# Lowering the place of the TensorE transposes in the attention stretch of a hybrid decoder layer

## The chip, the cores and the metric

The kernel runs on one core of a Trainium2 chip. The metric is device time in microseconds of one execution. Before the change the median of three runs is 2443.2 us (2442.11 to 2446.67).

## What is computed

One layer of a decoder over 2048 prompt rows and 8 decode rows of width 1024, all in float32. The stretch that the change touches is the first part: RMSNorm, one input projection into q, k, v and the convolution branch, banded attention with a window of 128 and sinks, and the causal convolution of width 31.

```python
z = rms_norm(x, norm_mix_g) @ w_in
q, k, v, cu = jnp.split(z, [Q_END, K_END, V_END], axis=-1)
q = rope(rms_norm(q.reshape(B, T, N_HEADS, HEAD_DIM), q_norm_g), pos)
k = rope(rms_norm(k.reshape(B, T, N_KV_HEADS, HEAD_DIM), k_norm_g), pos)
s = jnp.einsum('bnqkgd,bnjkd->bnkgqj', qb, kk) * ATTN_SCALE   # blocks of 128 queries, 256 keys
pr = sink_softmax_weights(s, mask, sink)
o = jnp.einsum('bnkgqj,bnjkd->bnqkgd', pr, vv)
a, g = jnp.split(cu, 2, axis=-1)
glu = a * jax.nn.sigmoid(g)
conv_o = jax.nn.silu(layer_norm(causal_dwconv(conv_ext, conv_w, conv_b), conv_ln_g, conv_ln_b))
h = x + jnp.concatenate([attn_o, conv_o], axis=-1) @ w_out
# then a gated ConvFFN (width 2816) and a gated per-layer embedding, each with its residual
```

## The kernel before

Every large product is made of three matmuls with operands split into a high and a low part (hi·hi, hi·lo, lo·hi; `mm3`, lines 195 to 197; the split is `hilo`, lines 212 and 213: a copy on ScalarE and a subtraction on VectorE).

The first 520 us or so work on the prompt in four quarters of 512 rows. A quarter consists of slots in an order written out by hand (`orders`): an "a" slot (`ag_unit`) is one 128-column piece of the convolution branch's projection, 24 matmuls of 512 columns; a "q" slot (`qkv_unit`) is the projection of one block of 128 rows to q, k and v, 24 matmuls of 512 and 24 of 256 columns (lines 820 to 825), and it starts a generator, `attn_block`, which is advanced slot by slot beside the projections. For one block `attn_block` does, a step per slot or two: transposes of q (four, line 596, tile qTp) and of k (two, line 599, tile kTp); scores of head group 0 (12 matmuls, line 621, tiles S); scores of head group 1; transposes of the probabilities of group 0 (two tiles PTp with four transposes each, line 648); the product with v (lines 659 to 662, tile O), beside it the transposes of group 1; the product of group 1. There are 16 blocks. `xn_k` transposes the normalized x of the next quarter (line 313, tile xT, four transposes for each 128 columns).

A matmul of scores contracts over a head's 64 dimensions only. It uses 64 of the 128 rows of the array: the even head of a pair the partitions 0 to 63, the odd head 64 to 127 (`rows = slice(par * 64, par * 64 + 64)`), each with a PSUM tile of its own. The loop issues the two in turn, even, odd, even, odd. In the order below, of two tiles S with neighbouring numbers, the lower number is the even head's. All transposes, projections and products with v contract over 128 rows.

All tiles of transposes and the product O rotate through one pool of two PSUM banks (`psT`, tag "T"); a buffer is free when `hilo` or a copy has read it.

The order on each engine is made when the program is built: a scheduler takes, among the instructions that it holds to be ready, the one with the lowest priority number. The number (`tc.cur_priority`) grows by one with each instruction that the program issues. The class `later(n)` raises it by n for the instructions in its body and takes it back behind them, so that these rank behind the next n instructions issued. It is already used at the layer norm's small matmuls (n = 60) and at a broadcast in the FFN stage. `bg` issues the convolution (line 411) in the background and puts the number back.

Of the kernel before, what the change touches and what calls it, by code (L numbers as in the profile page):

```python
# [33 lines left out]
def hybrid_layer_kernel(ctx: ExitStack, tc: tile.TileContext, I, O):  # L34
    nc = tc.nc
    DV, AC, GP, PE, SY = nc.vector, nc.scalar, nc.gpsimd, nc.tensor, nc.sync
# [29 lines left out]
    def ttile(name="T"):  # L66
        return psT.tile([128, 512], F32, tag="T", name=name)
# [100 lines left out]
    def col(src, c0):  # L168
        return src[:, :, c0:c0 + 128]
# [20 lines left out]
    for _ in range(4):  # L190
        for m in range(KD):
            W.add(col(w_gate, m * 128))

    def mm3(ps, wh, wl, xh, xl, first, last, more=False):
        PE.matmul(ps, wh, xh, start=first, stop=False, skip_group_check=more)  # L195
        PE.matmul(ps, wh, xl, start=False, stop=False, skip_group_check=more)  # L196
        PE.matmul(ps, wl, xh, start=False, stop=last, skip_group_check=more)  # L197

    def mm_tile(ps, hl, R, o, n):
        for k in range(KD):  # L200
            mm3(ps, hl[:, 0, k * 128:(k + 1) * 128], hl[:, 1, k * 128:(k + 1) * 128],
                R[k][:, 0, o:o + n], R[k][:, 1, o:o + n], k == 0, k == KD - 1)

    def mm_prod(ps, hl, c0, R, o, n, first):

        for k in range(4):
            w = slice(c0 + k * 128, c0 + (k + 1) * 128)
            mm3(ps, hl[:, 0, w], hl[:, 1, w], R[k][:, 0, o:o + n], R[k][:, 1, o:o + n],
                first and k == 0, k == 3, more=not first)

    def hilo(hi, lo, src):
        AC.copy(hi, src)  # L212
        DV.tensor_tensor(lo, src, hi.bitcast(F32), op=ALU.subtract)  # L213
# [11 lines left out]
    ident = const.tile([128, 128], F32, name="ident")  # L225
# [25 lines left out]
    xq = {}  # L251
# [56 lines left out]
    def xn_k(q, k):  # L308
        rt = r1_p.tile([128, 2, QT + NDEC], F32R, tag="r1", name="r1")
        g = gains[:, 0, k:k + 1]  # L310
        T = ttile("xT")
        for t in range(4):
            PE.transpose(T[:, t * 128:(t + 1) * 128], xq[q][t][:, k * 128:(k + 1) * 128], ident)
        AC.activation(rt[:, 0, :QT], T, func=AF.Identity, scale=g)
        DV.scalar_tensor_tensor(rt[:, 1, :QT], T, g, rt[:, 0, :QT].bitcast(F32), op0=ALU.mult, op1=ALU.subtract)
        if q == 3:
            xk = xdT.rearrange("p (b k) -> p b k", k=KD)[:, :, k]
            AC.activation(rt[:, 0, QT:], xk, func=AF.Identity, scale=g)
            DV.scalar_tensor_tensor(rt[:, 1, QT:], xk, g, rt[:, 0, QT:].bitcast(F32), op0=ALU.mult, op1=ALU.subtract)
        R1[q, k] = rt  # L320
# [13 lines left out]
    T = ttile("gT")  # L334
# [3 lines left out]
    for k in range(KD):  # L338
        xn_k(0, k)
    W.topup()  # L340
    T = ttile("cT")
# [46 lines left out]
    def conv_piece(conv_p, q):  # L388
# [22 lines left out]
                DV.scalar_tensor_tensor(co[c], t[:, i:i + QT], cvec[:, c, i:i + 1], co[c], op0=ALU.mult, op1=ALU.add)  # L411
                yield 610
        yield from layer_norm(conv_p, co, QT, 4, mixd[half], off)

    class later:


        def __init__(self, n):
            self.n = n

        def __enter__(self):
            tc.cur_priority += self.n

        def __exit__(self, *a):
            tc.cur_priority -= self.n

    def layer_norm(conv_p, co, n, ntt, dst, off):
        s = t_p.tile([128, QT], F32, tag="s", bufs=2, name="lns")[:, :n]
# [159 lines left out]
    def attn_block(b, pq, pkv):  # L588
        qn, kd, rs = qk_stage(b, pq, pkv)
        if b == 16:  # L590
            return
        yield 2
        qT = at_p.tile([128, 2, 4, 128], F32R, tag="qT", bufs=1, name="qT")
        T = ttile("qTp")
        for j in range(4):
            PE.transpose(T[:, j * 128:(j + 1) * 128], qn[:, j * 128:(j + 1) * 128], ident)
        T2 = ttile("kTp")
        for g in range(2):
            PE.transpose(T2[:, g * 128:(g + 1) * 128], kd[:, g].rearrange("p a d -> p (a d)"), ident)
        hilo(qT[:, 0].rearrange("p j t -> p (j t)"), qT[:, 1].rearrange("p j t -> p (j t)"), T)  # L600
        s = b % 2 + 1
        k2 = T2[:, :256].rearrange("p (g t) -> p g t", g=2)
        hilo(kTr[:, 0, :, s, :], kTr[:, 1, :, s, :], k2)
        yield 1
        den = at_p.tile([128, NH], F32, tag="den", bufs=2, name="den")
        mx = at_p.tile([128, NH], F32, tag="mx", bufs=2, name="mx")
        mv = mask[:, 0 if b else 1, :]
        Ps = {}

        def scores(g):  # L610
            P = at_p.tile([128, 4, 260], F32, tag="P", bufs=2, name="P")
            GP.tensor_copy(P[:, :, 256:257], sinkb[:, 4 * g:4 * g + 4].unsqueeze(2))
            Ps[g] = P
            S = [psS.tile([128, 2, 256], F32, tag="S", name="S") for _ in range(2)]

            for jj in range(2):
                j = 2 * g + jj
                for i, (a, e) in enumerate(((0, 1), (1, 0), (0, 0))):
                    for par in range(2):
                        rows = slice(par * 64, par * 64 + 64)  # L620
                        PE.matmul(S[par][:, jj, :], qT[rows, a, j, :],
                                  kTr[rows, e, g, s - 1:s + 1, :].rearrange("p a t -> p (a t)"),
                                  start=i == 0, stop=i == 2)
            for jj in range(2):
                for par in range(2):
                    h = 4 * g + 2 * jj + par
                    DV.tensor_tensor_reduce(out=P[:, 2 * jj + par, :256], in0=S[par][:, jj, :], in1=mv, scale=rs[:, h:h + 1],
                                            scalar=sinkb[:, h:h + 1], op0=ALU.add, op1=ALU.min, accum_out=mx[:, h:h + 1])
            for i in range(4):
                h = 4 * g + i  # L630
                AC.activation(P[:, i, :257], P[:, i, :257], func=AF.Exp, scale=-1.0, bias=mx[:, h:h + 1],
                              accum_out=den[:, h:h + 1])

        def normalize(g):
            g4 = slice(4 * g, 4 * g + 4)
            DV.reciprocal(den[:, g4], den[:, g4])
            for i in range(4):
                dn = den[:, 4 * g + i:4 * g + i + 1]
                AC.activation(Ps[g][:, i, :256], Ps[g][:, i, :256], func=AF.Identity, scale=dn)

        PTs = {}
        cks = (0, 1)

        def p_tr(g):
            for c in cks:
                T = ttile("PTp")
                for i in range(4):
                    PE.transpose(T[:, i * 128:(i + 1) * 128], Ps[g][:, i, c * 128:(c + 1) * 128], ident)
                PT = at_p.tile([128, 2, 512], F32R, tag="PT", bufs=2, name="PT")
                hilo(PT[:, 0], PT[:, 1], T)  # L650
                PTs[g, c] = PT

        def pv(g):
            Op = ttile("O")
            for c in cks:
                v2 = vts[b - 1 + c][:, g].rearrange("p a d -> p (a d)")
                PT = PTs.pop((g, c))
                if c == 0:
                    PE.matmul(Op, v2, PT[:, 0], start=True, stop=False)
                PE.matmul(Op[:64], v2[:, :64], PT[:, 1], start=False, stop=False)  # L660
                if c == 1:
                    PE.matmul(Op, v2, PT[:, 0], start=False, stop=True)
            ost = at_p.tile([128, 4, 128], F32, tag="ost", bufs=1, name="ost")
            AC.copy(ost.rearrange("p h t -> p (h t)"), Op)
            half, t0 = divmod(b * 128, HALF)
            for a in range(2):
                AC.dma_start(mixo[half][a, g * 256:(g + 1) * 256, t0:t0 + 128].rearrange("(h d) t -> d h t", d=HD),
                             ost[a * 64:(a + 1) * 64])

        scores(0)  # L670
        if s == 2:
            DV.tensor_copy(kTr[:, :, :, 0, :].rearrange("p a g t -> p (a g) t"),
                           kTr[:, :, :, 2, :].rearrange("p a g t -> p (a g) t").bitcast(F32))
        yield 1
        scores(1)
        normalize(0)
        yield 1
        p_tr(0)
        normalize(1)
        yield 1  # L680
        pv(0)
        p_tr(1)
        yield 1
        pv(1)
        vts.pop(b - 1, None)
# [185 lines left out]
    for q in range(4):  # L871
        ia = iq = 0
        L = len(orders[q])
        for si, ch in enumerate(orders[q]):
# [9 lines left out]
            else:  # L884
                t = 4 if ch == "d" else iq
# [30 lines left out]
        if q < 3:  # L916
            for k in range(2, KD):
                xn_k(q + 1, k)
# [563 lines left out]
    for a in range(0, NF, 4):  # L1482
        nf = min(4, NF - a)
        T = ttile("nfT")
# [62 lines left out]
```

## Time and profile before

| What | Value |
|---|---|
| median of three runs | 2443.2 us |
| profiled execution, time and span | 2447.62 us, 2445.7 us |
| mean granted TensorE clock | 0.984 |
| TensorE busy in the span | 2349.7 us (96%) |
| TensorE busy in 105 to 520 us | 392.6 of 415 us |
| VectorE, ScalarE busy in 105 to 520 us | 357.0 us, 273.9 us |
| granted clock in 105 to 520 us | 0.96 |
| matmuls of scores, transposes of probabilities | 384, 256 |

A row of the timeline gives the start in us from the span's start, the time in us, the engine, the line, what is written and read, the shape, and how many instructions in a row it stands for. Matmuls are pipelined and their ends are modelled, so that rows overlap: what an instruction costs TensorE is read from one start to the next. The windows view gives a stretch, its length, busy time of TensorE with its number of instructions, the granted clock, the share of the DMA engines and GB/s.

### The profile page before, as it was taken

What the parts mean: (1) busy time and instruction counts of PE and PEld (TensorE: products, weight loads), DVE (VectorE), ACT (ScalarE), POOL (GpSimd) and SP (SyncE); (2) the same over time, 40 slices, a digit from 0 to 9 for tenths busy, and PEclk for the clock granted to TensorE, in tenths of its full rate; (3) what the DMA queues carried; (4) which work ended last, traced back from release to release, by engine and by line L of the source; (5) the groups of instructions that cost most, each with busy time, mean ns of one, the idle gap of its engine ahead of it and who ended that gap; (6) DMA issues with size and microseconds to landing.
All of it is one profiled execution on the core that took longest, in us unless ns stands there. A gap on an engine that the chain in (4) does not pass through costs nothing.

```text
span 2445.7 us, 36659 instructions
## 1 busy us (share of the span) xinstructions
PE 2349.7 (96%) x13691; PEld 2039.8 (83%) x13691; DVE 1742.5 (71%) x2915; ACT 1188.9 (49%) x2186; POOL 323.5 (13%) x378
## 2 busy tenths in 40 slices
PE   8899999999899999999999997999999999999999
PEld 6677778877677777778778897999999999988878
DVE  4989879866799999779944569666666654465553
ACT  4566666665444444464333444444444543444443
POOL 3312232200311211110001104111111000000000
PEclk9989999999899999999999998999999999999999
DMA  8534422277322222255546651222222665666664
GB/s 291 173 116 130 137 95 78 79 219 231 98 87 83 86 88 86 90 170 187 195 159 194 205 179 44 84 81 79 75 77 78 215 211 180 205 215 205 201 175 114
DMA packets 357075, 348.19 MB, mean 142 GB/s; under 512 B 24414, under 2 KB 277784, under 8 KB 352770
## 3 DMA queue, kind: packets, MB, share of 16 engines
q1 hardware_dynamic: 336610, 333.25, 43.2%
q10 hardware_dynamic: 20288, 12.60, 1.8%
q8 instruction: 107, 1.75, 0.3%
q14 instruction: 70, 0.57, 0.1%
HBM read 271.61 MB, written 75.78 MB: 142 GB/s over the span
## 4 chain that ended last, share of the span: by engine, by line
PE 72%; DVE 14%; DMA 6%; ACT 3%; issue 2%; POOL 2%; SPq 0%; ACTq 0%; DVEq 0%; POOLq 0%
PE X L195 6%; PE X L197 6%; PE X L196 6%; PE fo L197 5%; PE fo L196 5%; PE fo L195 5%; DVE co L411 5%; PE Z L195 3%; PE Z L196 3%; PE Z L197 3%; PE pg L195 2%; PE pg L196 2%; PE pg L197 2%; PE wo L195 2%; PE wo L197 2%
## 5 line engine op out<-in xcount | busy, mean ns | idle before, releaser
L213 DVE TENSOR_TENSOR whl<-raw,whl 128x1024 fp32r<-128x1024 f32 (+1 forms) x314 | 361.6, 1152 | 236.0 <-ACT whl L212 235.4
L212 ACT CAST whl<-raw 128x1024 fp32r<-128x1024 f32 (+1 forms) x314 | 309.9, 987 | 251.3 <-PE fo L197 134.7
L411 DVE SCALAR_TENSOR_TENSOR co<-gi,cvec,co 128x512 f32<-128x512 f32 x480 | 364.4, 783 | 2.8
L195 PE MATMUL fo<-act,whl 128*128 128x512 f32 (+2 forms) x880 | 309.4, 352 | 2.6 <-DVE hs L1293 1.6
L197 PE MATMUL fo<-act,whl 128*128 128x512 f32 (+2 forms) x880 | 309.2, 351 | 0.9 <-DVE whl L213 0.9
L196 PE MATMUL fo<-act,whl 128*128 128x512 f32 (+2 forms) x880 | 309.7, 352 | 0.0
L195 PEld LDWEIGHTS fo<-act,whl 128*128 128x128 f32 x880 | 166.4, 189 | 18.8 <-DVE hs L1293 2.2
L195 PE MATMUL X<-T,whl 128*128 128x512 f32 (+2 forms) x528 | 173.0, 329 | 8.5 <-ACT whl L212 3.7
L197 PEld LDWEIGHTS fo<-act,whl 128*128 128x128 f32 x880 | 166.4, 189 | 17.0 <-DVE whl L213 1.1
L196 PEld LDWEIGHTS fo<-act,whl 128*128 128x128 f32 x880 | 166.4, 189 | 15.7 <-issue 0.2
L196 PE MATMUL X<-T,whl 128*128 128x512 f32 (+2 forms) x528 | 172.8, 327 | 5.0 <-POOL T L1119 4.2
L197 PE MATMUL X<-T,whl 128*128 128x512 f32 (+2 forms) x528 | 171.2, 324 | 0.6 <-DVE whl L213 0.6
L1216 POOL TENSOR_TENSOR snB<-snB 128x256 f32<-128x256 f32 (+1 forms) x66 | 85.5, 1296 | 503.1 <-ACT snB L1207 503.1
L1169 ACT ACTIVATE ft<-ft 128x512 f32<-128x512 f32 (+2 forms) x110 | 60.2, 548 | 165.1 <-DVE ft L1164 124.7
L195 PEld LDWEIGHTS X<-T,whl 128*128 128x128 f32 x528 | 101.7, 193 | 21.4 <-ACT snA L1180 5.4
L195 PE MATMUL ag<-r,whl 128*128 128x512 f32 (+2 forms) x320 | 116.2, 365 | 0.0
L196 PE MATMUL ag<-r,whl 128*128 128x512 f32 (+2 forms) x320 | 115.3, 361 | 0.0
L196 PEld LDWEIGHTS X<-T,whl 128*128 128x128 f32 x528 | 101.9, 193 | 13.9 <-POOL T L1119 5.1
L197 PE MATMUL ag<-r,whl 128*128 128x512 f32 (+2 forms) x320 | 113.4, 354 | 0.0
L1161 ACT ACTIVATE ft<-ext,fvec 128x512 f32<-128x512 f32 (+2 forms) x110 | 80.0, 729 | 64.2 <-DVE ext L1183 32.4
L197 PEld LDWEIGHTS X<-T,whl 128*128 128x128 f32 x528 | 101.8, 193 | 9.1 <-DVE whl L213 1.1
L196 PE MATMUL Z<-T,whl 128*128 128x512 f32 (+2 forms) x264 | 86.0, 326 | 6.3 <-POOL T L1119 6.3
(383 smaller groups left out, 6415.0 us busy)
## 6 DMA issues: line engine op xcount, KB each, us to landing
raw<-in_w_ffn_out SPq DMA_DIRECT2D x110, 512.0 KB
raw<-in_w_ffn_in SPq DMA_DIRECT2D x88, 512.0 KB
whl<-agd SPq DMA_DIRECT2D x24, 1024.0 KB
hs<-h SPq DMA_DIRECT2D x80, 256.0 KB
raw<-in_w_out SPq DMA_DIRECT2D x32, 512.0 KB
raw<-in_w_ple_gate SPq DMA_DIRECT2D x32, 512.0 KB
actd<-ft SPq DMA_DIRECT2D x44, 256.0 KB
act<-actd SPq DMA_DIRECT2D x44, 256.0 KB
```

The lines of the kernel that those rows point to most:

```text
L195: PE.matmul(ps, wh, xh, start=first, stop=False, skip_group_check=more)
L196: PE.matmul(ps, wh, xl, start=False, stop=False, skip_group_check=more)
L197: PE.matmul(ps, wl, xh, start=False, stop=last, skip_group_check=more)
L212: AC.copy(hi, src)
L213: DV.tensor_tensor(lo, src, hi.bitcast(F32), op=ALU.subtract)
L411: DV.scalar_tensor_tensor(co[c], t[:, i:i + QT], cvec[:, c, i:i + 1], co[c], op0=ALU.mult, op1=ALU.add)
L1161: AC.activation(t[:, :n], ext[:, 2 + o:2 + o + n], func=AF.Identity, scale=w2, bias=bi)
L1169: AC.activation(t[:, :n], t[:, :n], func=AF.Gelu)
L1216: GP.tensor_tensor(s3, s3, s5, op=ALU.add)
```

## The change

Three groups of transposes are issued inside `later(14)`: those of x in `xn_k` (in quarters 1 to 3, not in the first), those of q and k in `attn_block`, and those of the probabilities in `p_tr`. The tile k's transposes write is now allocated before q's transposes instead of behind them. The class itself only stands further up. No instruction is added or removed, and the functions called are the same.

```diff
@@ xn_k @@
         T = ttile("xT")
-        for t in range(4):
-            PE.transpose(T[:, t * 128:(t + 1) * 128], xq[q][t][:, k * 128:(k + 1) * 128], ident)
+        with later(14 if q else 0):
+            for t in range(4):
+                PE.transpose(T[:, t * 128:(t + 1) * 128], xq[q][t][:, k * 128:(k + 1) * 128], ident)
@@ attn_block @@
         T = ttile("qTp")
-        for j in range(4):
-            PE.transpose(T[:, j * 128:(j + 1) * 128], qn[:, j * 128:(j + 1) * 128], ident)
         T2 = ttile("kTp")
-        for g in range(2):
-            PE.transpose(T2[:, g * 128:(g + 1) * 128], kd[:, g].rearrange("p a d -> p (a d)"), ident)
+        with later(14):
+            for j in range(4):
+                PE.transpose(T[:, j * 128:(j + 1) * 128], qn[:, j * 128:(j + 1) * 128], ident)
+            for g in range(2):
+                PE.transpose(T2[:, g * 128:(g + 1) * 128], kd[:, g].rearrange("p a d -> p (a d)"), ident)
@@ p_tr @@
                 T = ttile("PTp")
-                for i in range(4):
-                    PE.transpose(T[:, i * 128:(i + 1) * 128], Ps[g][:, i, c * 128:(c + 1) * 128], ident)
+                with later(14):
+                    for i in range(4):
+                        PE.transpose(T[:, i * 128:(i + 1) * 128], Ps[g][:, i, c * 128:(c + 1) * 128], ident)
```

The lines of the changed kernel have other numbers: scores stand at 623, transposes of probabilities at 651, the products with v at 662 to 665, q and k's projection at 823 to 828, a branch's projection at 207 to 209, `hilo` at 224 and 225.

The order on TensorE is the same up to the first block's transposes of probabilities beside scores (105.9 us in the profiled execution) and the same again from 519 us on. Between, it differs mainly where a block's transposes of probabilities meet the next block's scores. TensorE's order there before, at the place that the profiled execution reaches at 189.9 us (S_1868 is the even head's tile, S_1869 the odd head's):

```order
L662 MATMUL O_1839<-PT_1763,v_1199 128x512
L648 MATMUL PTp_1848<-ident_121,P_1677 128x128 x4
L621 MATMUL S_1868<-kTr_317,qT_1771 128x256
L621 MATMUL S_1869<-kTr_317,qT_1771 128x256
L648 MATMUL PTp_1856<-ident_121,P_1677 128x128 x4
L621 MATMUL S_1868<-kTr_317,qT_1771 128x256
```

Four more pairs of scores and the projection's next matmul follow. The same place on TensorE now:

```order
L665 MATMUL O_1839<-PT_1763,v_1199 128x512
L623 MATMUL S_1868<-kTr_317,qT_1771 128x256
L651 MATMUL PTp_1848<-ident_121,P_1677 128x128
L623 MATMUL S_1869<-kTr_317,qT_1771 128x256
L623 MATMUL S_1868<-kTr_317,qT_1771 128x256
L651 MATMUL PTp_1848<-ident_121,P_1677 128x128
L623 MATMUL S_1869<-kTr_317,qT_1771 128x256
L651 MATMUL PTp_1848<-ident_121,P_1677 128x128
L623 MATMUL S_1868<-kTr_317,qT_1771 128x256
L651 MATMUL PTp_1848<-ident_121,P_1677 128x128
L623 MATMUL S_1869<-kTr_317,qT_1771 128x256
```

It goes on in this way until all eight transposes and twelve scores are out. A transpose stands alone between scores, and the even and the odd head's matmul are mostly apart. Thirteen blocks have this full alternation, six more a part of it. Over the stretch the places where a score stands directly before a transpose rise from 25 to 131, those where a transpose stands directly before a score from 39 to 135.

Where the transposes meet a projection, they move among its matmuls. TensorE's order some slots further on before, with the projection of the next block (pq and pk):

```order
L197 MATMUL ag_2009<-r1_1265,whl_1650 128x512
L648 MATMUL PTp_2039<-ident_121,P_1866 128x128 x4
L648 MATMUL PTp_2047<-ident_121,P_1866 128x128 x4
L820 MATMUL pq_2082<-wq0_325,r1_1077 128x512
L821 MATMUL pq_2082<-wq0_325,r1_1077 128x512
```

and now:

```order
L209 MATMUL ag_2009<-r1_1265,whl_1650 128x512
L651 MATMUL PTp_2039<-ident_121,P_1866 128x128
L651 MATMUL PTp_2047<-ident_121,P_1866 128x128
L823 MATMUL pq_2082<-wq0_325,r1_1077 128x512
L824 MATMUL pq_2082<-wq0_325,r1_1077 128x512
L825 MATMUL pk_2083<-wq0_325,r1_1077 128x256
L826 MATMUL pk_2083<-wq0_325,r1_1077 128x256
L827 MATMUL pq_2082<-wq0_325,r1_1077 128x512
L651 MATMUL PTp_2039<-ident_121,P_1866 128x128
L651 MATMUL PTp_2047<-ident_121,P_1866 128x128
```

The other four follow two by two between the next matmuls of the projection.

The order of VectorE follows: in the first of the two places the splits of the transposed probabilities (tile PT) go behind the first reader of the scores (line 627 before, 629 now). Before:

```order
L213 TENSOR_TENSOR PT_1853<-PTp_1848,PT_1853 128x512
L568 TENSOR_TENSOR qn_1906<-pk_1790,rs_1895 128x128
L627 ISA P_1866,mx_1865<-S_1868,mask_148,sinkb_149,rs_1589 128x256
L627 ISA mx_1865 128x1
L627 ISA P_1866,mx_1865<-S_1869,mask_148,sinkb_149,rs_1589 128x256
```

and now:

```order
L569 TENSOR_TENSOR qn_1906<-pk_1790,rs_1895 128x128
L575 TENSOR_TENSOR sq_1890<-pq_1789,tab_1900 128x512
L629 ISA P_1866,mx_1865<-S_1868,mask_148,sinkb_149,rs_1589 128x256
L629 ISA mx_1865 128x1
L225 TENSOR_TENSOR PT_1853<-PTp_1848,PT_1853 128x512
L225 TENSOR_TENSOR PT_1861<-PTp_1856,PT_1861 128x512
```

On ScalarE the issue of the attention output's DMA (line 667 before) moves from behind the first of the two copies PT to ahead of both in about ten blocks. SyncE issues the same DMAs; three of them change places with a neighbour, and GpSimd's order changes in seven neighbouring pairs.

More of the change, by code (lines that the diff above doesn't have):

```diff
@@ L192, in hybrid_layer_kernel, with __init__, __enter__, __exit__ @@
             W.add(col(w_gate, m * 128))
+    class later:
+        def __init__(self, n):
+            self.n = n
+        def __enter__(self):
+            tc.cur_priority += self.n
+        def __exit__(self, *a):
+            tc.cur_priority -= self.n
     def mm3(ps, wh, wl, xh, xl, first, last, more=False):
@@ L413, in conv_piece @@
         yield from layer_norm(conv_p, co, QT, 4, mixd[half], off)
[L415 to L425, printed above, removed]
     def layer_norm(conv_p, co, n, ntt, dst, off):
```

## The prediction

> **What bounds the kernel now.** I read the page's first part, then the windows of the stretch whose order changes, then TensorE's waits in it.
>
> ```profile
> PE 2349.7 (96%) x13691; PEld 2039.8 (83%) x13691; DVE 1742.5 (71%) x2915; ACT 1188.9 (49%) x2186; POOL 323.5 (13%) x378
> ...
> 105.00:520.00 415.00, 392.62 (x2381) 319.17 (x2381) 357.04 (x775) 273.88 (x644) 91.84 (x109) 0.96 0.36 115
> 520.00:2446.00 1926.00, 1870.15 (x10892) 1651.27 (x10890) 1316.40 (x2030) 859.47 (x1447) 193.29 (x224) 0.99 0.46 143
> ```
>
> TensorE bounds the whole and this stretch. From 105 to 520 us it is busy for 392.6 of 415 us; VectorE comes second with 357. What TensorE's sequence costs here is therefore paid in time, and at most 22 us of its waits can be given back. Behind 520 us the order is the same, so nothing is expected to change there.
>
> ```profile
> PE O L659 <- DVE qT L213: 6.1, 1, 6.1
> PE xT L313 <- DVE qT L213: 3.8, 1, 3.8
> PE lnv L455 <- DVE lnsq L448: 2.9, 1, 2.9
> PE qTp L596 <- DVE PT L213: 2.6, 3, 1.7
> ...
> PE PTp L648 <- ACT ost L664: 1.1, 2, 0.8
> PE xT L313 <- DVE PT L213: 1.0, 2, 0.6
> PE PTp L648 <- DVE r L315: 0.8, 1, 0.8
> PE PTp L648 <- DVE kTr L213: 0.7, 1, 0.7
> PE PTp L648 <- ACT P L639: 0.5, 2, 0.4
> ```
>
> These are the waits from 105 to 520 us (sum, times, longest). Those at moved transposes whose place really changes are qTp's and the five lower ones: 2.6 + 1.1 + 1.0 + 0.8 + 0.7 + 0.5 = 6.7 us. The xT wait of 3.8 us keeps its neighbours in the new order, and the two largest others are no transposes.
>
> **The price of neighbours on TensorE.** Since the work stays the same and only neighbours change, I price each kind of neighbour, from one start to the next.
>
> ```profile
> 105.76 0.40 PE L662 MATMUL O<-PT,v 128*128 128x512 f32 x1
> 106.00 0.60 PE L648 MATMUL PTp<-ident,P 128*128 128x128 f32 x4
> 106.53 0.38 PE L621 MATMUL S<-kTr,qT 64*128 64x256 f32 x2
> 106.84 0.66 PE L648 MATMUL PTp<-ident,P 128*128 128x128 f32 x4
> 107.43 0.85 PE L621 MATMUL S<-kTr,qT 64*128 64x256 f32 x10
> 108.21 0.39 PE L822 MATMUL pk<-wq,r 128*128 128x256 f32 x1
> ...
> 117.29 0.40 PE L662 MATMUL O<-PT,v 128*128 128x512 f32 x1
> 117.62 0.98 PE L621 MATMUL S<-kTr,qT 64*128 64x256 f32 x12
> 118.61 0.63 PE L596 MATMUL qTp<-ident,qn 128*128 128x128 f32 x4
> ...
> 132.32 0.60 PE L313 MATMUL xT<-ident,x 128*128 128x128 f32 x4
> 132.67 0.48 PE L196 MATMUL ag<-r,whl 128*128 128x512 f32 x1
> 132.98 0.39 PE L197 MATMUL ag<-r,whl 128*128 128x512 f32 x1
> 133.21 0.40 PE L195 MATMUL ag<-r,whl 128*128 128x512 f32 x1
> ...
> 378.61 1.09 PE L648 MATMUL PTp<-ident,P 128*128 128x128 f32 x8 [0.76 <-DVE r L315]
> 379.63 0.85 PE L621 MATMUL S<-kTr,qT 64*128 64x256 f32 x9
> ...
> 456.90 0.38 PE L621 MATMUL S<-kTr,qT 64*128 64x256 f32 x2
> 457.21 0.66 PE L648 MATMUL PTp<-ident,P 128*128 128x128 f32 x4
> ```
>
> - Transpose behind transpose: eight take 1.02 us (378.61 to 379.63), four 0.59 (106.84 to 107.43), both between scores; a further one costs (1.02 - 0.59)/4 = 0.11.
> - Transposes among projection matmuls: four take 0.35 (132.32 to 132.67) and the matmul behind them 0.31 instead of 0.23, together 0.43, again 0.11 each.
> - Transpose before a score: four behind O take 0.53 (106.00 to 106.53); less three at 0.11 the last takes 0.20.
> - Pair of scores before a transpose: 0.31 (106.53 to 106.84, and 456.90 to 457.21). In a run a pair takes 0.78/5 = 0.16, entry and exit included: its two matmuls run side by side.
> - First transpose behind scores: 0.59 - 0.53 = 0.06 more.
> - Score behind O: 0.33 (117.29 to 117.62) where a transpose waits 0.24 (105.76 to 106.00).
>
> So a change between 64-row scores and 128-row transposes costs TensorE time in each direction.
>
> **The sum, part by part.** The block at 106 us takes 2.21 us now (106.00 to 108.21) for eight transposes and twelve scores. In full alternation its eight transposes take 0.20 each and the scores before them 0.31 each: 8 x 0.51 = 4.08. The entry from O costs 0.09 more; the last score before the projection some 0.2 and the extra pair in one group 0.11. That is 4.5 us, 2.3 more; thirteen such blocks give 30. In the six partly alternating blocks three to four returns are added, each 0.51 less the 0.11 of a transpose and the 0.08 of half a pair, which are paid anyway, 0.3: 6 us. New borders between projections or O and scores, and even heads' matmuls that lose their partner, add 1: together **+37 us**.
>
> The trace has a transpose or a score alone between the others nowhere. A lone score may cost what a pair costs, since the pair starts together. Lower bound: the first return to scores is not paid at each exit, then an exit is nearer to the 0.2 that remains of the 0.99 at 118.61 when five pairs at 0.16 are taken off, the unit is 0.40, and over the 106 added returns (131 less 25) the sum is 37 - 106 x 0.11 = 25. Upper bound: each lone transpose pays the 0.06 as well, and 13 x 8 x 0.06 = 6 make it 43. I take 0.51, a pair directly between two groups of transposes being nearest.
>
> Transposes that move among projection matmuls cost nothing:
>
> ```profile
> 236.05 0.38 PE L648 MATMUL PTp<-ident,P 128*128 128x128 f32 x2
> 236.19 0.36 PE L825 MATMUL pk<-wq,r 128*128 128x256 f32 x1
> 236.39 0.39 PE L648 MATMUL PTp<-ident,P 128*128 128x128 f32 x2
> ```
>
> Two cost 0.14, and the 256-column matmul behind them 0.20 instead of 0.12 (a 0.08 like that above): 0.11 each, as in a group. The moves of xT, qTp and kTp are of this kind: 0 us, with the projection as cover.
>
> **Waits given back and added.** A transpose that came too early now stands behind scores that are ready: of 6.7 us I take 3 back, since in qTp's case the tile that it waits for is also split later. What is late next: a block's PT splits and its scores' last readers on VectorE, by the 2.3 us. The product with v that needs them stands a slot further on, behind 24 projection matmuls at 0.23, 5.6 us, and covers that; without that cover a block would lose up to 2.3 us. The DMA issues that ScalarE now does ahead of a copy delay that copy by their own time, with the transposes later still: 0. SyncE's three exchanges of neighbours: 0.
>
> **The clock.** Idle or thin work costs a second time here:
>
> ```profile
> 121.60:125.10 3.50, 0.41 (x4) 1.00 0.02 5
> 125.10:131.90 6.80, 6.80 (x29) 0.50 0.00 0
> 155.80:159.20 3.40, 1.98 (x13) 1.00 0.32 129
> 159.20:166.00 6.80, 6.80 (x24) 0.50 0.30 69
> 343.50:346.90 3.40, 1.70 (x8) 1.00 0.27 65
> 346.90:350.30 3.40, 0.00 (x0) 1.00 0.58 243
> 456.20:459.60 3.40, 3.40 (x29) 1.00 0.27 66
> 459.60:463.00 3.40, 3.40 (x22) 1.00 0.16 39
> ```
>
> Behind 3.4 us with four or thirteen instructions the granted clock is 0.50 for 6.8 us; behind a similar 3.4 us with eight mostly long ones, and behind 29, it stays 1.00. In alternation 3.4 us hold 3.4/0.51 = 6.7 units of one transpose and one or two scores, 13 to 17 short instructions: at the edge. A block lasts 4.5 us, so such a 3.4 us lies wholly in it in (4.5 - 3.4)/3.4, a third of the cases, more if an almost full one suffices. I take five of thirteen. Half clock for 3.4 to 6.8 us costs half of that, 2.5 on average: **+12 us**, bounds 0 and 13 x 2.5 = 32.
>
> The Trainium skill, page "TensorE: Matmul & The Clock Gate", Part 4: PE-mode transpose, says that transposes don't count as work for the clock gate. By that only the scores would count, all thirteen blocks would fall to half clock, and the clock's term would be 32. The trace is rather against it: behind 456.2 to 459.6 us, mostly transposes and scores, the clock stays whole.
>
> **The forecast.** 2447.6 (the profiled execution) + 37 + 12 - 3 = 2493.6. That execution is 4.4 us above the median of the runs shown, so the forecast for the median is **2489 us**, 1.9% slower.
>
> **The rivals.**
> - Half clock in all thirteen blocks: 2443.2 + 37 + 32 - 3 = 2509. For it: the units are as thin as the stretch at 155.8. Against: a 3.4 us stretch must lie in the block.
> - No half clock: 2443.2 + 37 - 3 = 2477. For it: TensorE is never idle in the alternation; against: the same stretch at 155.8 was 58% busy.
> - The returns are cheap (0.40 a unit or less) and no clock: 2443.2 + 25 - 3 = 2465.
> - Faster: the price of a change of neighbours is a wait for weights that can be loaded ahead when a single score, in half of the rows, lies between two transposes. Then neighbours cost nothing, 6.7 us of waits fall and the time is 2436. It decides if a border costs under 6.7/202 = 0.033 us (202 borders are added); the rows show 0.09 for the one direction and 0.15 for the other. Against it: the price of a pair is the same at 106 and at 457 us, with other data and other waits around.
> - The change does nothing: excluded, the order differs as it says.
>
> **How the numbers follow.** Forecast (2481 to 2499) 0.42; no half clock 0.20; all half 0.20; cheap returns 0.10; faster 0.05; within 0.2% 0.03. About 0.2%, 5 us, is what a measurement of this kernel can tell from no change. Slower is 0.92. The range takes in the rivals of the same sign: 2460 to 2516.
>
> **What would show it.** In the profile after: busy time of scores and transposes hardly tells, but starts do: a block from O to the projection lasts 4.5 us instead of 2.2, a transpose stands 0.31 behind a score and a score 0.20 behind a transpose. The stretch that now ends at 519 us ends near 565. Half clock shows as 0.50 right behind blocks, some five times more than before. It would be wrong if a lone score overlapped the transpose beside it, starts some 0.1 apart, or if O came to wait for PT in each block.

## The result

| | median | runs | lowest to highest | profiled execution |
|---|---|---|---|---|
| before | 2443.69 us | 5 | 2442.11 to 2446.67 | 2447.62 us |
| changed | 2500.31 us | 5 | 2488.80 to 2501.81 | 2499.28 us |

The ratio is 1.0228 with a 95% interval of 1.0206 to 1.0249: 2.3% slower. The forecast was 2489 us, within 2460 to 2516.

First the page's row of busy times of the changed kernel.

```profile
PE 2409.8 (96%) x13691; PEld 2067.7 (83%) x13691; DVE 1744.8 (70%) x2915; ACT 1190.3 (48%) x2186; POOL 318.1 (13%) x378
```

Then two of its windows: the stretch from the first to the last instruction on TensorE whose place changed, and the rest.

```profile
109.40:572.40 463.00, 447.51 (x2372) 343.76 (x2372) 357.75 (x771) 275.14 (x644) 90.09 (x109) 0.93 0.32 103
572.40:2497.50 1925.10, 1872.49 (x10896) 1652.60 (x10894) 1316.49 (x2030) 859.56 (x1448) 190.56 (x224) 0.99 0.46 143
```

The same stretch before, its window with TensorE alone:

```profile
106.00:519.30 413.30, 390.92 (x2374) 0.96 0.36 115
```

The stretch has grown from 413.3 to 463.0 us, TensorE's busy time in it by 56.6 us with the same instructions. VectorE and ScalarE are as busy as they were in a like stretch (357.0 and 273.9 us). The rest of the kernel takes 1925.1 us where it took 1926.4. So nearly all of it lies where the order changed.

One block of that stretch, the one whose order was shown, in the changed kernel's timeline:

```profile
197.85 0.39 PE L665 MATMUL O<-PT,v 128*128 128x512 f32 x1
198.16 0.38 PE L623 MATMUL S<-kTr,qT 64*128 64x256 f32 x1
198.48 0.33 PE L651 MATMUL PTp<-ident,P 128*128 128x128 f32 x1
198.73 0.39 PE L623 MATMUL S<-kTr,qT 64*128 64x256 f32 x2
199.05 0.33 PE L651 MATMUL PTp<-ident,P 128*128 128x128 f32 x1
199.31 0.38 PE L623 MATMUL S<-kTr,qT 64*128 64x256 f32 x1
199.62 0.33 PE L651 MATMUL PTp<-ident,P 128*128 128x128 f32 x1
199.88 0.38 PE L623 MATMUL S<-kTr,qT 64*128 64x256 f32 x1
...
202.47 0.33 PE L651 MATMUL PTp<-ident,P 128*128 128x128 f32 x1
202.73 0.38 PE L623 MATMUL S<-kTr,qT 64*128 64x256 f32 x1
203.04 0.50 PE L207 MATMUL ag<-r,whl 128*128 128x512 f32 x1
```

A lone score holds the transpose behind it up for 0.31 us (199.31 to 199.62), as a pair does (198.73 to 199.05: 0.32), and a lone transpose holds the score up for 0.26 (199.62 to 199.88). One unit is 0.57 us. The block lasts 4.88 us (198.16 to 203.04); in the profile before the block of the prediction took 2.21.

The waits in the changed stretch:

```profile
PE O L662 <- DVE qT L225: 6.3, 1, 6.3
PE xT L326 <- DVE qT L225: 3.4, 1, 3.4
PE PTp L651 <- DVE qT L225: 1.6, 1, 1.6
PE lnb L464 <- POOL lnr L234: 1.5, 1, 1.5
PE xdT L315 <- ACT xd L313: 1.4, 1, 1.4
PE PTp L651 <- ACT ost L667: 1.2, 1, 1.2
```

TensorE now is idle for 15.5 us of the stretch (463.0 less 447.5), before for 22.4 (413.3 less 390.9): 6.9 us came back. The two largest waits stayed.

The clock, in windows with TensorE alone: two blocks with what follows, and the block above with what follows.

```profile
231.30:235.10 3.80, 3.80 (x18) 1.00 0.29 69
235.10:242.00 6.90, 6.90 (x17) 0.51 0.13 24
...
500.10:504.80 4.70, 4.70 (x21) 1.00 0.23 56
504.80:508.20 3.40, 3.40 (x11) 0.50 0.08 24
198.20:203.00 4.80, 4.80 (x21) 1.00 0.23 56
203.00:206.40 3.40, 3.40 (x16) 1.00 0.00 0
```

After some blocks the granted clock halves, after others not. Of the thirteen fully alternating blocks five have a half clock that starts within them (at 235.1, 296.6, 337.5, 450.2 and 504.8 us) and one has it 0.55 us behind its end; another runs at half clock from its start, after the wait of 6.3 us. The mean clock of the stretch fell from 0.96 to 0.93; half clock holds for 65 of its 463 us, before for 31 of 413.

The five beginnings are 61.4, 41.0, 112.6 and 54.6 us apart: 18, 12, 33 and 16 steps of 3.413 us. In each of the ten profiles of this case every change of the granted clock lies on such a grid, and where the grid lies differs from execution to execution. The five blocks that fell fill 93% or more of one step; the six behind which the clock stays whole fill 84% or less of any, and the one that fell just behind its end fills 84%, so there is the edge.

### The profile page after: what moved, and what is told of

The parts are those of the page before. It is cut to its first block, busy times and chain, and to the rows that moved or that the text cites. A ratio compares the mean times of both kernels' runs of the same rounds, so it can differ in the third digit from the quotient of the medians.

```text
span 2497.5 us, 36660 instructions
## 1 busy us (share of the span) xinstructions
PE 2409.8 (96%) x13691; PEld 2067.7 (83%) x13691; DVE 1744.8 (70%) x2915; ACT 1190.3 (48%) x2186; POOL 318.1 (13%) x378
## 4 chain that ended last, share of the span: by engine, by line
PE 75%; DVE 11%; DMA 6%; ACT 3%; issue 2%; POOL 1%; SPq 0%; ACTq 0%; DVEq 0%; POOLq 0%
PE X L207 6%; PE X L208 6%; PE X L209 6%; PE fo L209 4%; PE fo L208 4%; PE fo L207 4%; DVE co L424 3%; PE Z L207 3%; PE Z L208 3%; PE Z L209 3%; PE S L623 2%; PE pg L207 2%; PE pg L209 2%; PE pg L208 2%; PE wo L207 2%
## 5 line engine op out<-in xcount | busy, mean ns | idle before, releaser
L207 PE MATMUL ag<-r,whl 128*128 128x512 f32 (+2 forms) x320 | 119.3, 375 | 0.0
L208 PE MATMUL ag<-r,whl 128*128 128x512 f32 (+2 forms) x320 | 118.8, 372 | 0.0
L209 PE MATMUL ag<-r,whl 128*128 128x512 f32 (+2 forms) x320 | 117.1, 366 | 0.0
```

## The experiments

The theory: a change between a matmul of 64 rows (scores) and one of 128 (transposes, projections) costs TensorE time in each direction, and the thin work that it makes halves the clock at times. I call such a change a border, and this the border theory. The first rival is lateness: whatever is put off is late for the engine behind it. The second: the price is one of alternation as such, whatever the rows. In the expectations the counts of borders include one with a transpose of the decode rows, so they are higher by one than those told ahead of the prediction.

**Which of the three groups of transposes.** Only those of the probabilities keep the lower place:

```diff
@@ xn_k @@
-        with later(14 if q else 0):
+        with later(0):
@@ attn_block @@
-        with later(14):
+        with later(0):
             for j in range(4):
```

> Only the transposes of the probabilities keep the lower place; those of x, q and k stand as before. TensorE's order has the same 132 + 135 borders between scores and transposes as the whole change. Border theory (a change between 64-row scores and 128-row transposes costs TensorE about 0.2 us in each direction, thin work halves the clock on top): as slow as the whole change, 2490 to 2502 us. Lateness theory (every transpose that is put off makes its split and the next product late, x, q and k's too): part of the loss goes, 2455 to 2485 us.

Measured: 2499.18 us (2496.57 to 2501.83), ratio to the kernel before 1.0228, 1.0213 to 1.0243. The whole loss is there with this part alone. The order is that of the whole change, too: in the trace TensorE, VectorE, GpSimd and SyncE go through the same operations and tiles (buffer numbers left out) in the same sequence.

So the two profiles show one order against two positions of the clock's grid. The ninth of the thirteen blocks, at 403.7 to 408.6 us in the changed kernel, fills 60% and 83% of two steps, and the clock stays whole:

```profile
402.38:405.79 3.41, 3.41 (x16) 1.00 0.51 151
405.79:409.21 3.42, 3.42 (x16) 1.00 0.95 322
409.21:412.62 3.41, 3.41 (x26) 1.00 0.01 2
```

In this run it lies at 407.2 to 412.4 us and fills a whole step, and the next is at half clock:

```profile
408.16:411.57 3.41, 3.41 (x17) 1.00 0.96 380
411.57:414.99 3.42, 3.42 (x12) 0.50 0.26 69
```

The tenth is the other way round: it fell in the changed kernel (96% of a step) and not here (81%). Here the six that fell fill 89% or more, the others at whole clock 84% or less.

The other way round, only the transposes of x, q and k keep it:

```diff
@@ p_tr @@
-                with later(14):
+                with later(0):
                     for i in range(4):
```

> Only the transposes of x, q and k get the lower place; those of the probabilities stand as before. 26 + 39 borders, as before. Border theory: no change, 2443 us within 5. Lateness theory: slower, 2455 us or more.

Measured: 2444.08 us beside 2444.65 before, ratio 1.000, 0.9989 to 1.001. The trace says why: TensorE, VectorE, GpSimd and SyncE go through the same operations and tiles in the same sequence as before. Lowering x, q and k's transposes by 14 alone puts nothing off, so this run doesn't test what their lateness costs, and lateness of the probabilities is still open. Of the three groups of the change, that of the probabilities alone changes the order.

**The place as a dose.** The number 14 is replaced in all three groups by 8, 28, 20 and 40:

```diff
-        with later(14 if q else 0):
+        with later(28 if q else 0):
...
-                with later(14):
+                with later(28):
                     for i in range(4):
```

> The whole change with 8 in place of 14. 55 + 68 borders, 58 more than before where the change has 202 more. Border theory: 58 x 0.21 = 12 us slower, with a half clock or two 2453 to 2465 us. Lateness theory (loss in proportion to the place): 8/14 of 57 us, 2476 us.

Measured: 2451.48 us beside 2444.65, ratio 1.0027, 1.0015 to 1.004. Slower, by less than both theories said, and far from the 2476 of lateness.

> The whole change with 28 in place of 14: transposes are put off twice as far and come out behind the scores, among projection matmuls. 31 + 8 borders, 26 fewer than before. Border theory: 26 x 0.2 = 5 us saved, 1 to 3 us more at other borders, waits of some us either way: 2435 to 2447 us. Lateness theory: twice the loss, 2500 us or more, up to 2555.

Measured: 2442.15 us beside 2444.65, ratio 0.999, 0.998 to 1.0. Put off twice as far, the transposes cost nothing at all. At the place that was shown above they now come out together, behind all twelve scores:

```profile
187.64 0.97 PE L623 MATMUL S<-kTr,qT 64*128 64x256 f32 x12
188.54 1.09 PE L651 MATMUL PTp<-ident,P 128*128 128x128 f32 x8
```

Lateness falls with that: it asked for 2500 us or more. Whether it is really faster than before can't be told.

> The whole change with 20 in place of 14: 115 + 96 borders, 146 more than before. Border theory: 146 x 0.2 = 29 us, and half clock in part of the blocks, 5 to 12 us, less 3 to 7 us of waits: 2470 to 2485 us, faster than the whole change with 14. Lateness theory: slower than with 14, 2525 us.

Measured: 2462.54 us beside 2445.49, ratio 1.007, 1.0055 to 1.0085. Faster than with 14, as the borders say, and lower than the range that I gave. Two things were missized. TensorE's window of the stretch:

```profile
109.10:536.40 427.30, 418.02 (x2373) 0.97 0.35 111
```

TensorE is idle for only 9.3 us, 13.1 less than before: the wait of 6.1 us for O is gone here, for a reason that stays open. And the half clock that I expected didn't come: it holds for 24 us of the stretch. A typical block of this kernel in the timeline:

```profile
193.10 0.73 PE L623 MATMUL S<-kTr,qT 64*128 64x256 f32 x7
193.77 0.33 PE L651 MATMUL PTp<-ident,P 128*128 128x128 f32 x1
...
196.06 0.66 PE L651 MATMUL PTp<-ident,P 128*128 128x128 f32 x4
196.47 0.48 PE L207 MATMUL ag<-r,whl 128*128 128x512 f32 x1
```

and the windows of this block and of what follows it:

```profile
193.10:196.50 3.40, 3.40 (x22) 1.00 0.33 78
196.50:199.90 3.40, 3.40 (x17) 1.00 0.01 1
```

It has nine borders, begins with seven scores in a row, ends with four transposes and lasts 3.37 us; the clock stays whole.

> The whole change with 40 in place of 14: 21 + 4 borders, 40 fewer than before; the borders of scores with projections rise from 41 to 53, and 16 score matmuls more lose their partner. Border theory: 40 x 0.17 = 7 us saved, 2 + 2 lost, waits from transposes that come too late 0 to 5: 2438 to 2446 us. Lateness theory: over 2500 us.

Measured: 2450.35 us beside 2445.49, ratio 1.0017, 1.0006 to 1.0028. It has the fewest borders and isn't faster. Its profiled execution has more waits: in 105 to 520 us q's transposes wait 4.5 us for the splits PT on VectorE and the probabilities' 4.4 us for ScalarE's copy of O, where before it was 2.6 and 1.1. Here some lateness may begin to show; no run tests that further.

Side by side, in us, from the profiled executions (one each), the last column from the medians:

| place | borders scores to transposes + back | stretch | idle TensorE in it | half clock in it | median less before's |
|---|---|---|---|---|---|
| before | 25 + 39 | 413.3 | 22.4 | 31 | 0 |
| 8 | 54 + 68 | 419.0 | 18.1 | 31 | +6.8 |
| 14 | 131 + 135 | 463.0 | 15.5 | 65 | +56.6 |
| 20 | 114 + 96 | 427.3 | 9.3 | 24 | +17.1 |
| 28 | 30 + 8 | 407.9 | 22.5 | 24 | -2.5 |
| 40 | 20 + 4 | 415.3 | 28.2 | 24 | +4.9 |

Per border: with 8, 5.7 us of stretch and 4.3 of waits given back over 58 borders, 0.17. With 20, 14.0 us, 13.1 of waits and 3.4 (half of the 7 us less half clock) over 146 borders, 0.21. With 14, 49.7 us and 6.9 of waits, less 13 to 17 for 34 us more half clock, over 202 borders, 0.20 to 0.22. Where borders are added, the loss follows them, not the place.

Where they are taken away, the same account gives back less: 2 us with 28 and 0.3 with 40, for 26 and 40 borders fewer. The table leaves out the scores' borders with projections and with O, where rows change as well. The traces have 41 of them before and with 8, 63 with 14, 51 with 20, 57 with 28 and 53 with 40. Counted together, 10 are saved with 28, again 0.2 each, and 28 with 40, where the account stays open. One execution each carries some us of chance besides: the run with only x, q and k's transposes has the order of before, and its stretch is 408.5 us, with 20 at half clock.

**The disputed price itself.** Scores that contract over all 128 partitions, first in the kernel before, then in the changed one, each in its own unchanged order:

```diff
-                        rows = slice(par * 64, par * 64 + 64)
+                        rows = slice(0, 128)
```

> The kernel before with scores that contract over all 128 partitions instead of 64, for the even and the odd head alike. It leaves out the separation of the two heads of a pair (each gets the sum of both scores); the order on TensorE is the same as before. Two matmuls of a pair no longer run side by side: 384 at 0.118 us are 45 us where scores now take about 35 with their exits; in exchange no border is paid (some 13 us). All theories: 2440 to 2455 us.

Measured: 2444.95 us beside 2445.49, ratio 0.999, 0.9981 to 1.0. The total is the same, as expected. What the lost pairs, the saved borders and the clock have in it, this run doesn't tell apart: half clock holds for 17 us of the stretch in its profile.

> The changed kernel with the same 128-partition scores (the heads of a pair are not separated), in the changed kernel's order with its 267 borders. Border theory (the price is that of a change between 64-row and 128-row matmuls, and the half clock comes from the thin work that it makes): the loss goes away, within 6 us of the kernel before with 128-partition scores. Rival (the price is one of alternation as such: new weights each time, transposes one by one, splits that come late, PSUM): 30 us or more above that kernel.

Measured: 2445.66 us beside 2445.49, ratio 1.0005, 0.9995 to 1.0015; 0.7 us above the kernel before with these scores. All 57 us are gone, with the same 267 borders in the order, the same single transposes and the same splits behind them. The same block as above, in this kernel's timeline:

```profile
189.01 0.40 PE L665 MATMUL O<-PT,v 128*128 128x512 f32 x1
189.24 0.28 PE L623 MATMUL S<-kTr,qT 128*128 128x256 f32 x1
189.36 0.27 PE L651 MATMUL PTp<-ident,P 128*128 128x128 f32 x1
189.39 0.48 PE L623 MATMUL S<-kTr,qT 128*128 128x256 f32 x2
189.71 0.27 PE L651 MATMUL PTp<-ident,P 128*128 128x128 f32 x1
189.74 0.37 PE L623 MATMUL S<-kTr,qT 128*128 128x256 f32 x1
189.94 0.27 PE L651 MATMUL PTp<-ident,P 128*128 128x128 f32 x1
...
191.35 0.36 PE L623 MATMUL S<-kTr,qT 128*128 128x256 f32 x1
191.55 0.40 PE L207 MATMUL ag<-r,whl 128*128 128x512 f32 x1
```

A unit of a transpose and a score is 0.23 us (189.71 to 189.94) instead of 0.57, the block 2.31 (189.24 to 191.55) instead of 4.88. What costs is that the rows of the array change, not that two kinds of work alternate. The Trainium skill, page "TensorEngine Tiling (Array Packing)", Key Properties, says that a change of the tiling mode, not just of the tile, makes TensorE drain. The trace agrees in that each such change costs time, some 0.2 us here; that a drain is what is waited for, no row shows.

What the rows do show is when the weights are loaded (PEld). With 128-partition scores a load stands ahead of its matmul, beside the work before it: 189.71 for the score at 189.74, 189.85 for the transpose at 189.94.

```profile
189.71 0.19 PEld L623 LDWEIGHTS S<-kTr,qT 128*128 128x128 f32 x1
189.85 0.14 PEld L651 LDWEIGHTS PTp<-ident,P 128*128 128x128 f32 x1
```

In the changed kernel the loads stand at 199.62 and 199.88, where the transpose and the score themselves are shown to start:

```profile
199.62 0.14 PEld L651 LDWEIGHTS PTp<-ident,P 128*128 128x128 f32 x1
199.88 0.18 PEld L623 LDWEIGHTS S<-kTr,qT 64*128 64x128 f32 x1
```

So across a border no weights are loaded ahead. In the whole trace, at full clock, the median lead of the load is 2 ns at borders in either direction; with 128-partition scores it is 96 ns for a transpose behind a score and 26 ns for a score behind a transpose. What holds the load back stays open.

The split between borders and clock was not made by a run of its own: 128-partition scores take away both. It stands on the rows.

## Why the prediction was right, point by point

**TensorE bounds the stretch: right.** With the same order on every engine and scores of 128 rows the loss is gone, so it is TensorE's own time. The rest of the kernel didn't change but for chance: 1.3 us less behind, 3.4 us more ahead of the first changed instruction (109.39 instead of 106.00), where a half clock at 102.0 to 105.4 us stands that the profiled execution before didn't have there.

**The price of neighbours: right, at its upper bound.** The prediction took 0.51 us for a unit, from pairs and groups. Its upper bound was that each lone transpose pays the 0.06 as well, a unit of 0.57. It does: 0.20 and 0.06 make the 0.26 of the timeline. A lone score costs 0.31, what a pair costs, as taken. At 4.88 us, the length at whole clock, the thirteen blocks cost 2.7 each, 35 us, and with the prediction's 6 and 1 us for the rest, which were not measured apart, the term is 42, not 37; the 40 to 44 us of the account by borders fit that. This is the term that was missized.

**The rival of a faster kernel, in which weights can be loaded ahead: wrong.** It needed a border under 0.033 us; a border costs some 0.2, and its weights are not loaded ahead.

**Moves among projection matmuls cost nothing: right.** The run with only x, q and k's transposes lowered doesn't show it, since nothing moves there, and the prediction counted moves of xT, qTp and kTp, which their own lowering doesn't make. But with 40 nearly all transposes of the probabilities stand among projection matmuls, and TensorE's busy time in the stretch is 387.1 us (415.3 less 28.2), not above the 390.9 of before. The account that stays open there leaves room for some us.

**Waits: too small.** 6.9 us came back, I took 3. Of the 6.7 us that I counted as movable some 4 came back, a new wait of PTp of 1.6 taken off; the rest is the layer norm's wait of 2.9 (lnv), which is gone and was not in my sum. The xT wait and the wait for O stayed, as said. The cover for late splits of PT held: no new wait of O for them is in the list.

**The clock: right, and near in size.** Five of thirteen were taken; five blocks and one just behind its end show it, and 34 us more half clock in all. At half clock a unit takes 0.91 us in the changed kernel, here:

```profile
235.30 0.58 PE L623 MATMUL S<-kTr,qT 64*128 64x256 f32 x1
235.81 0.47 PE L651 MATMUL PTp<-ident,P 128*128 128x128 f32 x1
236.21 0.58 PE L623 MATMUL S<-kTr,qT 64*128 64x256 f32 x1
```

So (0.91 - 0.57)/0.91, 37% of such time, is lost, and half of it where projections run: 34 us cost 13 to 17, where 12 was taken. Where a block falls against the grid decides, as the prediction's third of the cases had it, so this part differs from execution to execution: in the run with only the probabilities' transposes lowered, half clock holds for 75 us of the stretch, with the same order.

**The rival from the Trainium skill's rule**, page "TensorE: Matmul & The Clock Gate", Part 4: PE-mode transpose, that transposes don't count as busy in the same way (by the prediction all thirteen blocks would fall): five or six fell, and the block at 198.2 us, 4.8 us of nothing but transposes and scores, was followed by a whole clock until 206.4. As I had applied the rule, the trace is against it.

**The sum.** The forecast's 46 us on the profiled execution stand against 51.7 (2499.28 less 2447.62): borders 5 more, clock about 3 more, waits 4 less, outside of the stretch 2. The other 5 us of the medians' 56.6 are in the profiled executions' own place: that of before lies 3.9 us above its median, that of the change 1.0 below. The profile that I started from was slower than all five runs, and I carried its 4.4 us over as a constant.

## What to carry to other kernels

When work that uses a part of the array's rows stands beside work that uses all of them, price the borders from one start to the next before a scheduler is given freedom to mix them: here a border costs 0.2 us, twice a transpose, and 202 of them, with the half clock that their thin work brings, cost 2.3%. Lower a priority far enough to get a group out of the other's way, or not at all; 28 was harmless, 8 and 20 cost a little, 14 the most. And read the order that comes out, since the number says nothing on how finely the two will be mixed, or whether anything moves at all: lowering two of the three groups alone moved nothing.

## What the runs showed that I had not expected

- A single 64-row score costs as much as two that run side by side when a transpose follows (0.31 and 0.32 us), so mixing loses the pair's overlap as well.
- The granted clock halves while TensorE is shown busy without a gap: 231.3 to 235.1 us is busy for 3.80 of 3.80 us, and 0.51 follows. Busy time of modelled ends doesn't tell thin work. Nor do instructions alone: the block at 198.2 us has 21 in 4.8 us, fewer in a us than the 18 in 3.8 here, and the clock behind it stays whole. It fills at most 83% of a step of the grid; the other fills a whole one.
- A block must be thin as well as fill a step of the grid. In the kernel with 20, none of the twelve blocks of 3.4 us (nine borders) has a half clock behind it, though one fills 97% of a step (149.5 to 152.8 us). Of its four blocks of 4.4 to 4.6 us with fifteen borders two fell (half clock from 405.5 and 456.7 us); these two fill a whole step, the others 81% and 76%.
